# Two mixers paced more slowly, their columns read out by ScalarE, and four products moved ahead of the points where they must end

## The chip, the core and the metric

One Trainium2 chip, one of its cores. The metric is the device time of one execution of the whole program in microseconds (us), median of three runs.

## The reference

Two transformer-like blocks over 256 tokens of width 2048, all in float32. Only the first half of the first block matters here:

```
h = rms_norm(x, mix_norm)
u, q, f, i, og, cx, v, o, ig, fg, gates = split(h @ w_in)
y_a = s5_mixer(u, ...)                 # linear recurrence in 32 groups of 64 complex states, GELU, GLU
y_b = hgrn2_mixer(q, f, i, og, ...)    # gated linear attention, 6 heads of 128
y_c = mlstm_mixer(cx, v, o, ig, fg, ...)
merged = sigmoid(g_a) * (y_a @ wb_a) + sigmoid(g_b) * (y_b @ wb_b) + sigmoid(g_c) * (y_c @ wb_c)
x = x + merged @ w_out                 # then the feed-forward part, and the second block
```

In `hgrn2_mixer`, `q` becomes `silu(q)`, `f` becomes `lb + (1 - lb) * sigmoid(f)`, `k = 1 - f`, and `log f` is summed over time.

## The kernel before

**Products.** Every large product streams its weights from HBM in tiles of 128 x 1024 (two blocks of 128 rows by 512 columns). ScalarE rounds a tile to `hi`, VectorE takes `lo = raw - hi`, and TensorE runs the product in three parts (`mmA` and `mmB`, L362 to L380). One tile is one step of a product. Each of `raw`, `hi` and `lo` has three buffers, and the tile of step s + 2 is split while step s is multiplied. A product accumulates in one of two PSUM buffers called `mm`.

**The order.** Everything is written into the engines' instruction streams in a fixed order; each engine runs its own stream in order. `block1` runs these products: the columns of S5 and the first 512 of HGRN2 together (16 steps, the list `first`), two more products for the HGRN2 columns `q` and `f` (8 steps each), then HGRN2's values and gate (`nat("w_b")`, 24 steps), mLSTM's columns (`w_b` 8 and `w_c` 8 steps), then the merge gates by column block c and branch b (`gates(c)`, three products of 8 steps), `nat("w_d")` (24), and the branch products (`branch(c, b)`, 2 steps for S5's branch, 3 for the others). Numbered from the first, step 32 ends the HGRN2 columns, step 72 ends `w_c`, step 96 ends `gates(0)`, step 144 ends `w_d`. A step of `w_c` has tiles of 584 columns.

**Background.** The three mixers are Python generators. After each step `bg.pump()` lets them write some of their instructions between the products. How much is set by two meters that add up planned costs for VectorE and ScalarE (no measured times), every instruction of the engine counted, those of the products too:

```
RATE, CAP = 2.6, 2
self.V = Meter(nc.vector, 0.066, 1.042e-3, 0.13)   # fixed, per element of a row, extra below 100
self.S = Meter(nc.scalar, 0.2, 0.84e-3)
self.cv = min(self.cv + self.rate - (self.vec.t - self.seen[0]), CAP)   # in pump; ca alike
while self.cv > 0 and self.ca > 0:                 # the first task in the list that is ready
```

A generator's `yield` ends a piece; `yield 1` or `yield 2` gives up that many pumps; `yield self.hold("m2")` waits for a PSUM buffer (`m2` has one, `m1` two). The list of tasks is in the order S5's constants, S5, HGRN2 (short tasks that finish a product go ahead of them), so HGRN2 gets what S5 leaves. `bg.finish(task)` writes all the rest of a task at that point, without regard to the credit: nothing of the next product stands between those instructions.

**S5** (`s5`, from L722): four groups g of two halves. One half is four small products into `s5px` (L742), seven pieces on VectorE (twelve operations on 128 x 512 and four scans on 128 x 256) and products into `s5py` (L775, L776). GpSimd builds the tables of cosines and sines (`s5_table`), of which group g + 1 is asked for when group g begins. At the end come a GELU, the GLU product (`s5g`, L790) with weights loaded by a DMA of GpSimd's queue into two buffers of the pool `a4`, a sigmoid and `ya`. `bg.finish(t_s5)` stands after `gates(0)`, at step 96.

**HGRN2** (`hg`, from L811): the gates' arithmetic; two diagonal products (L849); seven levels for block lengths 1 to 64, each with an Exp on ScalarE, up to four operations on VectorE and two groups of products (L878); then the part across 128 tokens (L900), the output (L914, L915), a norm per head, and transposes (L948) that give `yb`. `bg.finish(t_hg)` stands after `nat("w_d")`, at step 144. mLSTM starts when HGRN2 has ended.

**The first columns.** `first[1]`, in one of the two `mm` buffers, and the next product are multiplied by the tokens' factor `R` (1 / rms) straight out of PSUM on VectorE, after `bg.finish(t_st)`, where the factor is there.

Of the kernel before, what the change touches and what calls it, by code (L numbers as in the profile page):

```python
# [11 lines left out]
AF = mybir.ActivationFunctionType  # L12
OP = mybir.AluOpType
# [5 lines left out]
class Meter:  # L19


    def __init__(self, eng, fixed, per, chain=0.0):
        self.eng, self.fixed, self.per, self.chain, self.t = eng, fixed, per, chain, 0.0

    def __getattr__(self, name):
        f = getattr(self.eng, name)

        def call(*a, **k):
            n = 1
            for x in (*a, *k.values()):  # L30
                if hasattr(x, "shape"):
                    m = 1
                    for d in x.shape[1:]:
                        m *= d
                    n = max(n, m)
            self.t += self.fixed + self.per * n + (self.chain if n < 100 else 0.0)
            return f(*a, **k)  # L37

        return call
# [503 lines left out]
class Mixers(Net):  # L543
# [60 lines left out]
    def s5_consts(self, a4f):  # L604

        V, nc = self.V, self.nc
        s = lambda k, n=16: self.p5.tile([128, n], F32, name=k)
        bc = a4f([128, 1024], F32, "s5bc")
        bt, ct = bc[:, 0:512], bc[:, 512:1024]
        lr, li = self.col("lam_re"), self.col("lam_im")  # L610
        yield 4
        dt = yield from self.exp16(self.col("log_dt"), "dt")
        lrd, th, den, t, ar, ai, cr, ci = (s(k) for k in ("lrd", "th", "den", "t16", "ar", "ai", "cr", "ci"))
        V.tensor_mul(th, li, dt)
        V.tensor_mul(lrd, lr, dt)
        yield
        cs, sn = yield from self.sincos(th, self.p5, [128, 16], "sc")
        mag = self.mag = yield from self.exp16(lrd, "mag")
        yield
        self.nc.sync.dma_start(bt, self.A["s5_b"])  # L620
        self.nc.sync.dma_start(ct, self.A["s5_c"])
        V.tensor_mul(t, lr, lr)
        V.tensor_mul(den, li, li)
        V.tensor_add(den, den, t)
        V.reciprocal(den, den)
        ex = a4f([128, 2, 16, 32], F32, "s5ex")
        cc = self.s5cc = a4f([128, 2, 16, 32], F32, "s5cc")
        self.G.memset(ex, 0.0)
        self.G.memset(cc, 0.0)
        yield 2  # L630
        V.tensor_mul(ar, mag, cs)
        V.tensor_mul(ai, mag, sn)
        V.tensor_scalar(ar, ar, -1.0, None, op0=OP.add)
        V.tensor_mul(cr, ar, lr)
        V.tensor_mul(t, ai, li)
        V.tensor_add(cr, cr, t)
        V.tensor_mul(cr, cr, den)
        V.tensor_mul(ci, ai, lr)
        V.tensor_mul(t, ar, li)
        V.tensor_sub(ci, ci, t)  # L640
        V.tensor_mul(ci, ci, den)
        yield

        self.pw = s("pw", 256).rearrange("p (z k n) -> p z k n", z=2, k=8)
        V.tensor_copy(self.pw[:, 0, 0], cs)
        V.tensor_copy(self.pw[:, 1, 0], sn)
        t2 = s("t162")
        for k in range(7):
            if k % 3 == 0:
                yield  # L650
            c, z = self.pw[:, 0, k], self.pw[:, 1, k]
            V.tensor_mul(t, c, c)
            V.tensor_mul(t2, z, z)
            V.tensor_sub(self.pw[:, 0, k + 1], t, t2)
            V.scalar_tensor_tensor(self.pw[:, 1, k + 1], c, 2.0, z, op0=OP.mult, op1=OP.mult)
        self.s5_base()
        self.s5_t0 = self.s5_table(0)
        yield

        b4 = bt.rearrange("p (z n q) -> p z n q", z=2, n=16)  # L660
        c4 = ct.rearrange("p (z n q) -> p z n q", z=2, n=16)
        t1 = s("s5t", 256).rearrange("p (n q) -> p n q", n=16)
        for g in range(2):
            h = slice(g * 64, g * 64 + 64)
            q = slice(g * 16, g * 16 + 16)
            crb = cr[h, :, None].to_broadcast([64, 16, 16])
            cib = ci[h, :, None].to_broadcast([64, 16, 16])
            V.tensor_mul(ex[h, 0, :, q], b4[h, 0], crb)
            V.tensor_mul(t1[h], b4[h, 1], cib)
            V.tensor_sub(ex[h, 0, :, q], ex[h, 0, :, q], t1[h])  # L670
            yield
            V.tensor_mul(ex[h, 1, :, q], b4[h, 1], crb)
            V.tensor_mul(t1[h], b4[h, 0], cib)
            V.tensor_add(ex[h, 1, :, q], ex[h, 1, :, q], t1[h])
            V.tensor_copy(cc[h, 0, :, q], c4[h, 0])
            V.tensor_scalar(cc[h, 1, :, q], c4[h, 1], -1.0, None, op0=OP.mult)
        bb = self.s5bb = a4f([128, 2, 4, 128], F32, "s5bb")
        for z in range(2):
            yield self.hold("m1")
            ps = self.m1([128, 4, 128])  # L680
            for g in range(4):
                nc.tensor.transpose(ps[:, g], ex[:, z, 4 * g:4 * g + 4].rearrange("p a b -> p (a b)"), self.ident)
            yield 1
            V.tensor_copy(bb[:, z], ps)
            self.drop("m1")
# [36 lines left out]
    def s5(self, u):  # L722

        V, S, nc = self.V, self.S, self.nc
# [5 lines left out]
        for g in range(4):  # L730
            if g < 3:
                tabs[g + 1] = self.s5_table(g + 1)
            C, Sn = tabs.pop(g)
            yield self.hold("m1")
            py = self.m1([128, 256], "s5py")
            for hf in range(2):
# [8 lines left out]
                c, s = C[:, 2 * hf:2 * hf + 2], Sn[:, 2 * hf:2 * hf + 2]  # L745
# [11 lines left out]
                for j in range(2):  # L757
                    p = 4 * g + 2 * hf + j
# [13 lines left out]
                for j in range(2):  # L772
                    q = (2 * hf + j) * 32
                    p = 4 * g + 2 * hf + j
# [33 lines left out]
    def a6(self, shape, dt=F32, name="a6"):  # L808
        return self.a6p.tile(shape, dt, tag="a6", name=name)

    def hg(self, qr, fr):  # L811
        V, S, G, nc = self.V, self.S, self.G, self.nc
        lb, om = self.small([128, 6], "lb"), self.small([128, 6], "om")

        src = self.col("hg_lb")
# [13 lines left out]
        V.memset(kh, 0.0)  # L829
        yield  # L830
        for h in range(6):
            V.tensor_scalar(fr[:, h], fr[:, h], om[:, h:h + 1], lb[:, h:h + 1], op0=OP.mult, op1=OP.add)
        yield
        k = self.a6([128, 6, 256], name="hgk")
        V.tensor_scalar(k, fr, -1.0, 1.0, op0=OP.mult, op1=OP.add)
        yield
        V.tensor_scalar(fr, fr, 1e-19, None, op0=OP.max)
        S.activation(fr, fr, AF.Ln)
        P = fr
# [3 lines left out]
        for t in range(2):  # L843
# [3 lines left out]
            ps = self.m2([128, 6, 128])  # L847
# [6 lines left out]
        for j, b in enumerate((1, 2, 4, 8, 16, 32, 64)):  # L854
# [19 lines left out]
            for t in range(2):  # L874
                yield self.hold("m1")
                ps = self.m1([128, 6, 64])
# [21 lines left out]
        ps = self.m2([128, 6, 128])  # L898
# [9 lines left out]
        for t in range(2):  # L908
            yield self.hold("m2")
            ps = self.m2([128, 6, 128])  # L910
# [183 lines left out]
class Block1(Mixers):  # L1094
# [14 lines left out]
    def order(self):  # L1109

        p = self.plan
# [5 lines left out]
        p("w_c", 0, 8, w=292)  # L1117
        p("w_g", 0, 48)
        p("w_d", 0, 24)
        for c in range(4):  # L1120
            if c > 1:
                p("w_g", 24 * c, 24)
            p("w_br", 5 * c, 5)
        p("w_br", 20, 12)
        pp = self.pair_plan
# [52 lines left out]
    def block1(self):  # L1178
# [9 lines left out]
        X = XT(self)  # L1188
# [73 lines left out]
        def s5():  # L1262
            yield lambda: t_st[3]
            V.tensor_mul(u, first[0], Rb(4))
            self.drop("m2")
            yield from self.s5(u)

        t_s5 = bg.add(s5())
        qr = self.a6([128, 6, 256], name="hgq")
        fr = self.a6([128, 6, 256], name="hgf")  # L1270
        ps = self.prodA("w_a", X, 16)
        bg.finish(t_st)
        r, R = st["r"], st["R"]
        V.tensor_mul(qr[:, 0:4], first[1], Rb(4))
        V.tensor_mul(qr[:, 4:6], ps[:, 0:2], Rb(2))
        V.tensor_mul(fr[:, 0:2], ps[:, 2:4], Rb(2))
        ps = self.prodA("w_a", X, 16)
        V.tensor_mul(fr[:, 2:6], ps, Rb(4))
        self.hg_v = self.hg_gate = self.ml_v = self.ml_gate = None
        t_hg = bg.add(self.hg(qr, fr))  # L1280


        def nat(name, fn, make, row, done):
# [39 lines left out]
        ps = self.prodA("w_b", X, 16)  # L1323
# [14 lines left out]
        for z in range(2):  # L1338
            V.tensor_mul(gt[0:4, z], ps[32 * z:32 * z + 4, 2], R[32 * z:32 * z + 4])

        def gates(c):
            out = []
            for b in range(3):
                ps = self.prodB("w_g", X, 16)
                g = self.a4([128, 2, 512], name="gate")
                for t in range(2):
                    S.activation(g[:, t], ps[:, t], AF.Sigmoid, scale=r[:, t:t + 1])
                out.append(g)
            return out

        def branch(c, b):

            yh, yl = getattr(self, ("ya", "yb", "yc")[b])
            ps = self.prodB("w_br", lambda k: (yh[:, k], yl[:, k]), (4, 6, 6)[b])
            V.tensor_mul(g[c][b], ps, g[c][b])
        g = [gates(0)]
        bg.finish(t_s5)
        s5p.close()
        lp = mixp.enter_context(tc.tile_pool(name="late", bufs=1, reuse_waits="tile"))
        self.late = lambda shape, name: lp.tile(shape, F32, name=name)  # L1360
        t_ml = bg.add(self.ml(cx, gt, lambda: t_hg[3]))
        g.append(gates(1))
        nat("w_d", None, self.late, "ml_norm", ml_done)
        bg.finish(t_hg)
        for c in range(4):
            if c > 1:
                g.append(gates(c))
            for b in range(2):
                branch(c, b)
            G.tensor_add(g[c][0], g[c][0], g[c][1])  # L1370
            g[c][1] = None
        bg.finish(t_ml)
# [808 lines left out]
```

## Time and profile before

| | us |
|---|---|
| median of three runs | 3503.44 (3500.94 to 3505.87) |
| the profiled execution, its own time | 3505.45 |
| its span, first to last instruction | 3503.6 |

The span is what the views below show; the profiled execution's time lies 1.85 us above it. Times in a view are from the span's start. Matmul ends are modelled, so what counts for TensorE is when instructions start and what it waited for. In the names of tiles buffer numbers are left out, and every VectorE and ScalarE instruction has the helper's line L37, so these go by tile: `lo<-raw,hi` is the split of a weight tile, `mm` a product's PSUM tile, `m` a small PSUM tile.

### The profile page before, as it was taken

How to read it: one execution, taken by the hardware profiler on the slowest of the kernel's cores; microseconds unless marked ns; L12 is line 12 of the kernel's file. 1: busy time of each engine (PE TensorE's matmuls, PEld its weight loads, DVE VectorE, ACT ScalarE, POOL GpSimd, SP SyncE). 2: the span in 40 equal slices, each digit the busy share in tenths (PEclk: the TensorE clock that was granted, in tenths of full speed). 3: DMA queues.
4: the chain of work that ended last, by engine and by line, in shares of the span. 5: the costliest groups of instructions: out<-in, count | busy, mean ns of one | idle time of the engine just before them, and what ended most of it. 6: DMA issues, size and time to landing. Idle time of an engine off the chain costs nothing.

```text
span 3503.6 us, 47474 instructions
## 1 busy us (share of the span) xinstructions
PE 3465.1 (99%) x18330; PEld 2976.7 (85%) x18330; DVE 2426.0 (69%) x3216; ACT 1717.5 (49%) x2103; POOL 240.6 (7%) x288
## 2 busy tenths in 40 slices
PE   8999999999999999999999999999999999999999
PEld 8788888888888888888888889988888888888887
DVE  7897575566776577657769998876666666666665
ACT  4435543445554455555554456654444444444454
POOL 5520000000000000003203000000000000000000
PEclk9999999999999999999999999999999999999999
DMA  7444554565566555665555556667666666667765
GB/s 236 149 148 163 176 176 140 194 207 184 188 198 199 186 192 193 192 192 180 159 163 178 183 182 209 214 195 214 202 202 202 203 202 201 202 202 216 217 186 180
DMA packets 236314, 665.85 MB, mean 190 GB/s; under 512 B 77956, under 2 KB 78404, under 8 KB 234168
## 3 DMA queue, kind: packets, MB, share of 16 engines
q1 hardware_dynamic: 230952, 637.49, 57.1%
q10 hardware_dynamic: 2448, 15.22, 1.4%
q0 software_dynamic: 2688, 10.12, 1.0%
q8 instruction: 143, 2.34, 0.3%
q14 instruction: 83, 0.68, 0.1%
HBM read 645.97 MB, written 16.78 MB: 189 GB/s over the span
## 4 chain that ended last, share of the span: by engine, by line
PE 92%; DVE 4%; DMA 1%; issue 1%; ACT 0%; DVEq 0%; ACTq 0%
PE mm L362 33%; PE mm L393 23%; PE mm L366 16%; PE mm L395 12%; PE mm L377 2%; DVE lo L37 2%; PE m L2028 2%; PE mm L380 1%; DMA raw<-in_w_u_dram 1%; PE m L496 1%; PE m L878 0%; DVE s L37 0%; PE m L1038 0%; DVE cand L37 0%; DVE e L37 0%
## 5 line engine op out<-in xcount | busy, mean ns | idle before, releaser
L37 DVE TENSOR_TENSOR lo<-raw,hi 128x1024 fp32r<-128x1024 f32 (+1 forms) x1169 | 1428.5, 1228 | 754.3 <-ACT hi L37 748.2
L37 ACT ACTIVATE hi<-raw 128x1024 fp32r<-128x1024 f32 (+1 forms) x1185 | 1245.3, 1054 | 1290.3 <-PE mm L362 716.9
L393 PE MATMUL mm<-xt,hi 128*128 128x512 f32 x3712 | 898.6, 392 | 0.0
L393 PEld LDWEIGHTS mm<-xt,hi 128*128 128x128 f32 x3712 | 679.5, 188 | 129.0
L395 PEld LDWEIGHTS mm<-xt,lo 128*128 128x128 f32 x3712 | 478.1, 191 | 21.0 <-DVE lo L37 2.9
L395 PE MATMUL mm<-xt,lo 128*128 128x256 f32 x3712 | 491.2, 284 | 2.0 <-DVE lo L37 2.0
L362 PE MATMUL mm<-hi,wl 128*128 128x512 f32 x1024 | 400.0, 391 | 1.9 <-DVE wl L37 1.9
L362 PE MATMUL mm<-hi,wh 128*128 128x512 f32 x928 | 361.6, 390 | 0.0
L362 PE MATMUL mm<-hi,x 128*128 128x512 f32 x1152 | 289.7, 394 | 1.0 <-ACT hi L37 1.0
L362 PEld LDWEIGHTS mm<-hi,x 128*128 128x128 f32 x1152 | 213.5, 188 | 48.8 <-issue 3.9
L366 PE MATMUL mm<-lo,wh 128*128 128x512 f32 x928 | 248.2, 389 | 0.0
L362 PEld LDWEIGHTS mm<-hi,wl 128*128 128x128 f32 x1024 | 193.1, 189 | 42.1 <-DVE wl L37 2.2
L362 PEld LDWEIGHTS mm<-hi,wh 128*128 128x128 f32 x928 | 174.3, 188 | 36.1
L366 PEld LDWEIGHTS mm<-lo,wh 128*128 128x128 f32 x928 | 174.2, 188 | 36.1
L362 PE MATMUL mm<-hi,xt 128*128 128x512 f32 x752 | 186.9, 391 | 0.1
L37 DVE TENSOR_TENSOR resid<-resid,mm 128x1024 f32<-128x1024 f32 x84 | 102.5, 1220 | 99.3 <-PE mm L366 99.3
L362 PEld LDWEIGHTS mm<-hi,xt 128*128 128x128 f32 x752 | 140.4, 188 | 29.2 <-issue 0.5
L366 PE MATMUL mm<-lo,x 128*128 128x512 f32 x576 | 155.1, 391 | 5.5 <-DVE lo L37 5.5
L362 PE MATMUL mm<-hi,acth 128*128 128x512 f32 x352 | 137.3, 390 | 0.0
L362 PE MATMUL mm<-hi,actl 128*128 128x512 f32 x352 | 137.0, 389 | 0.0
L366 PEld LDWEIGHTS mm<-lo,x 128*128 128x128 f32 x576 | 107.6, 188 | 30.7 <-DVE lo L37 8.5
L366 PE MATMUL mm<-lo,xt 128*128 128x512 f32 x376 | 100.6, 389 | 0.0
(566 smaller groups left out, 3530.1 us busy)
## 6 DMA issues: line engine op xcount, KB each, us to landing
raw<-in_w_u_dram SPq DMA_DIRECT2D x256, 512.0 KB, 4.1
raw<-in_w_v_dram SPq DMA_DIRECT2D x256, 512.0 KB, 4.2
raw<-in_w_up_dram SPq DMA_DIRECT2D x176, 512.0 KB, 4.0
raw<-in_w_g_dram SPq DMA_DIRECT2D x96, 512.0 KB, 3.3
raw<-in_w_dn_dram SPq DMA_DIRECT2D x88, 512.0 KB, 3.4
raw<-in_w_o_dram SPq DMA_DIRECT2D x64, 512.0 KB, 3.4
raw<-in_w_b_dram SPq DMA_DIRECT2D x32, 512.0 KB, 3.5
raw<-in_w_br_dram SPq DMA_DIRECT2D x32, 512.0 KB, 3.4
```

The lines of the kernel that those rows point to most:

```text
L37: return f(*a, **k)
L362: nc.tensor.matmul(ps[:, t, :n], x[:, t * 128:t * 128 + 128], hi[:, i, :n], start=first and i == z == 0, stop=False)
L366: nc.tensor.matmul(ps[:, t, :n], X(k0 + i)[0][:, t * 128:t * 128 + 128], lo[:, i, :n], start=False, stop=last and i == kk - 1)
L377: nc.tensor.matmul(ps[:, c, :], hi[:, i, sl[c]], x, start=first and i == z == 0 and c % 2 == 0, stop=False, **kw)
L380: nc.tensor.matmul(ps[:, c, :], lo[:, i, sl[c]], X(k0 + i)[0], start=False, stop=last and i == kk - 1, **kw)
L393: nc.tensor.matmul(ps[:, c], hi[:, i, sl[c]], X.both(k0 + i), start=first and i == 0, stop=last and i == kk - 1, **kw)
L395: nc.tensor.matmul(ps[:, c, 256:], lo[:, i, sl[c]], X(k0 + i)[0], start=False, stop=False, **kw)
L496: self.nc.tensor.transpose(ps[:, c, t * 128:t * 128 + 128], src(t)[:, c * 128:c * 128 + 128], self.ident)
L2028: nc.tensor.matmul(ps[n][:, i], AB[:, 1, i], AB[:, 0, i], start=True, stop=True)
```

## The change

HGRN2's columns leave PSUM by ScalarE copies without the factor; `hg` multiplies them by `R` in SBUF as its first two pieces. The affine of `f` (six operations) and `k = 1 - f` go from VectorE to ScalarE. The meter of VectorE counts every cost 1.3 times from the end of the powers in `s5_consts` until S5's group 3 begins. Two products of `gates(1)` (16 steps) move ahead of `bg.finish(t_s5)`, and `branch(0, 0)` and `branch(1, 0)` (2 steps each) ahead of `bg.finish(t_hg)`; the weights' stream in `order` follows.

```diff
--- before.py
+++ after.py
@@ -21,6 +21,7 @@
 
     def __init__(self, eng, fixed, per, chain=0.0):
         self.eng, self.fixed, self.per, self.chain, self.t = eng, fixed, per, chain, 0.0
+        self.k = 1.0
 
     def __getattr__(self, name):
         f = getattr(self.eng, name)
@@ -33,7 +34,7 @@
                     for d in x.shape[1:]:
                         m *= d
                     n = max(n, m)
-            self.t += self.fixed + self.per * n + (self.chain if n < 100 else 0.0)
+            self.t += self.k * (self.fixed + self.per * n + (self.chain if n < 100 else 0.0))
             return f(*a, **k)
 
         return call
@@ -653,6 +654,7 @@
             V.tensor_mul(t2, z, z)
             V.tensor_sub(self.pw[:, 0, k + 1], t, t2)
             V.scalar_tensor_tensor(self.pw[:, 1, k + 1], c, 2.0, z, op0=OP.mult, op1=OP.mult)
+        V.k = 1.3
         self.s5_base()
         self.s5_t0 = self.s5_table(0)
         yield
@@ -730,6 +732,8 @@
         for g in range(4):
             if g < 3:
                 tabs[g + 1] = self.s5_table(g + 1)
+            else:
+                V.k = 1.0
             C, Sn = tabs.pop(g)
             yield self.hold("m1")
             py = self.m1([128, 256], "s5py")
@@ -808,8 +812,12 @@
     def a6(self, shape, dt=F32, name="a6"):
         return self.a6p.tile(shape, dt, tag="a6", name=name)
 
-    def hg(self, qr, fr):
+    def hg(self, qr, fr, Rb):
         V, S, G, nc = self.V, self.S, self.G, self.nc
+        V.tensor_mul(fr, fr, Rb(6))
+        yield
+        V.tensor_mul(qr, qr, Rb(6))
+        yield
         lb, om = self.small([128, 6], "lb"), self.small([128, 6], "om")
 
         src = self.col("hg_lb")
@@ -829,11 +837,11 @@
         V.memset(kh, 0.0)
         yield
         for h in range(6):
-            V.tensor_scalar(fr[:, h], fr[:, h], om[:, h:h + 1], lb[:, h:h + 1], op0=OP.mult, op1=OP.add)
+            S.activation(fr[:, h], fr[:, h], AF.Identity, scale=om[:, h:h + 1], bias=lb[:, h:h + 1])
         yield
         k = self.a6([128, 6, 256], name="hgk")
-        V.tensor_scalar(k, fr, -1.0, 1.0, op0=OP.mult, op1=OP.add)
-        yield
+        S.activation(k, fr, AF.Identity, scale=-1.0, bias=1.0)
+        yield 1
         V.tensor_scalar(fr, fr, 1e-19, None, op0=OP.max)
         S.activation(fr, fr, AF.Ln)
         P = fr
@@ -1117,9 +1125,12 @@
         p("w_c", 0, 8, w=292)
         p("w_g", 0, 48)
         p("w_d", 0, 24)
-        for c in range(4):
-            if c > 1:
-                p("w_g", 24 * c, 24)
+        p("w_br", 0, 2)
+        p("w_br", 5, 2)
+        p("w_br", 2, 3)
+        p("w_br", 7, 3)
+        for c in (2, 3):
+            p("w_g", 24 * c, 24)
             p("w_br", 5 * c, 5)
         p("w_br", 20, 12)
         pp = self.pair_plan
@@ -1266,18 +1277,19 @@
             yield from self.s5(u)
 
         t_s5 = bg.add(s5())
+
         qr = self.a6([128, 6, 256], name="hgq")
         fr = self.a6([128, 6, 256], name="hgf")
+        S.activation(qr[:, 0:4], first[1], AF.Copy)
         ps = self.prodA("w_a", X, 16)
+        S.activation(qr[:, 4:6], ps[:, 0:2], AF.Copy)
+        S.activation(fr[:, 0:2], ps[:, 2:4], AF.Copy)
+        ps = self.prodA("w_a", X, 16)
+        S.activation(fr[:, 2:6], ps, AF.Copy)
         bg.finish(t_st)
         r, R = st["r"], st["R"]
-        V.tensor_mul(qr[:, 0:4], first[1], Rb(4))
-        V.tensor_mul(qr[:, 4:6], ps[:, 0:2], Rb(2))
-        V.tensor_mul(fr[:, 0:2], ps[:, 2:4], Rb(2))
-        ps = self.prodA("w_a", X, 16)
-        V.tensor_mul(fr[:, 2:6], ps, Rb(4))
         self.hg_v = self.hg_gate = self.ml_v = self.ml_gate = None
-        t_hg = bg.add(self.hg(qr, fr))
+        t_hg = bg.add(self.hg(qr, fr, Rb))
 
 
         def nat(name, fn, make, row, done):
@@ -1338,9 +1350,9 @@
         for z in range(2):
             V.tensor_mul(gt[0:4, z], ps[32 * z:32 * z + 4, 2], R[32 * z:32 * z + 4])
 
-        def gates(c):
+        def gates(c, bs=range(3)):
             out = []
-            for b in range(3):
+            for b in bs:
                 ps = self.prodB("w_g", X, 16)
                 g = self.a4([128, 2, 512], name="gate")
                 for t in range(2):
@@ -1353,20 +1365,22 @@
             yh, yl = getattr(self, ("ya", "yb", "yc")[b])
             ps = self.prodB("w_br", lambda k: (yh[:, k], yl[:, k]), (4, 6, 6)[b])
             V.tensor_mul(g[c][b], ps, g[c][b])
-        g = [gates(0)]
+        g = [gates(0), gates(1, range(2))]
         bg.finish(t_s5)
         s5p.close()
         lp = mixp.enter_context(tc.tile_pool(name="late", bufs=1, reuse_waits="tile"))
         self.late = lambda shape, name: lp.tile(shape, F32, name=name)
         t_ml = bg.add(self.ml(cx, gt, lambda: t_hg[3]))
-        g.append(gates(1))
+        g[1] += gates(1, range(2, 3))
         nat("w_d", None, self.late, "ml_norm", ml_done)
+        branch(0, 0)
+        branch(1, 0)
         bg.finish(t_hg)
         for c in range(4):
             if c > 1:
                 g.append(gates(c))
-            for b in range(2):
-                branch(c, b)
+                branch(c, 0)
+            branch(c, 1)
             G.tensor_add(g[c][0], g[c][0], g[c][1])
             g[c][1] = None
         bg.finish(t_ml)
```

## Rows read from the trace of the kernel before

**Rows 1.** The page's part 1: engine, busy us, share of the span, instructions.

```profile
PE 3465.1 (99%) x18330; PEld 2976.7 (85%) x18330; DVE 2426.0 (69%) x3216; ACT 1717.5 (49%) x2103; POOL 240.6 (7%) x288
```

**Rows 2.** Windows, all engines: length, busy of each, then PEclk, DMA share, GB/s.

```profile
82.15:85.19 3.04, 0.00 (x1) 0.03 (x1) 3.04 (x4) 0.00 (x0) 2.96 (x4) 0.88 0.26 94
85.19:93.69 8.50, 8.50 (x49) 8.50 (x49) 4.34 (x5) 1.82 (x2) 8.34 (x9) 0.64 0.38 103
112.65:158.40 45.75, 39.17 (x171) 28.92 (x169) 41.35 (x46) 17.90 (x19) 27.76 (x29) 1.00 0.42 136
158.40:195.93 37.53, 37.01 (x180) 28.77 (x180) 32.92 (x45) 19.57 (x22) 0.00 (x0) 1.00 0.57 184
195.93:247.90 51.97, 49.17 (x407) 46.12 (x405) 48.98 (x61) 17.68 (x20) 22.48 (x26) 1.00 0.43 128
```

**Rows 3.** Timeline of TensorE, 85 to 139 us: start, length, group, idle before it.

```profile
85.19 3.76 PE L377 MATMUL mm<-x,hi 128*128 128x256 f32 x16 [3.04 <-DVE hgq L37]
...
104.01 2.08 PE L377 MATMUL mm<-x,hi 128*128 128x256 f32 x16
...
106.89 2.08 PE L377 MATMUL mm<-x,hi 128*128 128x256 f32 x16
...
138.90 1.19 PE L366 MATMUL mm<-lo,x 128*128 128x512 f32 x4 [1.69 <-DVE lo L37]
```

**Rows 4.** Timeline of TensorE: S5's first half, its last group and its end.

```profile
99.97 1.14 PE L742 MATMUL s5px<-u,s5bb 32*128 32x256 f32 x8
...
273.90 1.14 PE L742 MATMUL s5px<-u,s5bb 32*128 32x256 f32 x8
...
318.29 0.63 PE L775 MATMUL s5py<-s5sr,s5cc 128*32 128x256 f32 x4
...
323.04 7.17 PE L790 MATMUL s5g<-s5y,glu 128*128 128x256 f32 x32 [0.71 <-ACT s5y L37]
```

**Rows 5.** Timeline of TensorE: HGRN2's levels 4 and 64, its last transposes.

```profile
335.52 1.45 PE L878 MATMUL m<-hgqh,hgkh 128*128 128x64 f32 x12
...
400.91 1.45 PE L878 MATMUL m<-hgqh,hgkh 128*128 128x64 f32 x12
...
453.65 0.60 PE L948 MATMUL m<-cols,hgo 128*128 128x128 f32 x4
```

**Rows 6.** One S5 half on VectorE: all instructions of the window, then `lo` alone.

```profile
250.21:266.05 15.84, 15.67 (x21) 1.00 0.54 170
...
250.21:266.05 15.84, 6.07 (x5) 1.00 0.54 170
```

**Rows 7.** Groups by form on VectorE, 401 to 456 us: count, busy, mean ns.

```profile
L37 DVE TENSOR_TENSOR hgnq<-hgo 128x1536 f32<-128x1536 f32 x1 | 1.8, 1751 | 0.0
...
L37 DVE TENSOR_TENSOR hgqh<-hgqh,hgq 128x768 f32<-128x768 f32 x1 | 0.9, 950 | 0.0
...
L37 DVE SCALAR_TENSOR_TENSOR hgny<-hgnt,hgny 128x12 f32<-128x12 f32 x3 | 0.5, 171 | 0.1
```

**Rows 8.** Groups by form on ScalarE, 401 to 456 us.

```profile
L37 ACT ACTIVATE hgo<-m 128x768 f32<-128x768 f32 x2 | 1.6, 812 | 3.7 <-PE m L915 3.7
```

**Rows 9.** Timeline of VectorE, 119 to 160 us.

```profile
119.60 1.22 DVE L37 TENSOR_TENSOR hgf<-mm,R 128x1024 f32<-128x1024 f32 x1
...
134.03 2.83 DVE L37 TENSOR_TENSOR hgq<-hgq,hgkh 128x1536 f32<-128x1536 f32 x1
...
158.19 2.02 DVE L37 TENSOR_SCALAR hgf<-hgf,om,lb 128x256 f32<-128x256 f32 x6
```

**Rows 10.** Timeline of ScalarE, S5's GELU and its sigmoid.

```profile
321.93 1.06 ACT L37 ACTIVATE s5y<-s5y 128x1024 f32<-128x1024 f32 x1 [2.08 <-DVE s5y L37]
...
330.25 1.56 ACT L37 ACTIVATE s5z<-s5g,cols 128x256 f32<-128x256 f32 x4 [4.69 <-PE s5g L790]
```

**Rows 11.** DMA issues, 280 to 330 us: count, KB, median us to landing.

```profile
glu<-in_w_glu_dram POOLq DMA_DIRECT2D x2, 512.0 KB, 5.3
```

## The prediction, made before the change was run

> **What bounds the kernel now.** I read the page's part 1 first: TensorE is busy 99% of the span [rows 1], so a change around the mixers moves the time only where TensorE waits for them. The windows of the first 480 us then show where that is. TensorE is idle 3.04 us at 82.15, runs the next 8.50 us at a mean clock of 0.64, and is idle 6.58, 0.52 and 2.80 us in the three windows from 112.65 to 247.90 (length less busy) [rows 2]. The timeline says for what: at 85.19 the fourth product waited for `hgq`, VectorE's multiplication that empties the PSUM buffer; at 138.90 it waited for `lo`, the split that VectorE delivers late [rows 3]. After that it waits 0.71 us for the GELU at S5's end [rows 4], and from there to the feed-forward part it is dense. VectorE is the second limit up to 247.90: 41.35 of 45.75 us and 48.98 of 51.97 us are busy, while ScalarE has more than half of its time free [rows 2].
>
> The clock's price comes from the same rows. A step of this kind takes 2.88 us (104.01 to 106.89) [rows 3]; the two steps from 85.19 took 8.50 us in place of 5.76, so the half-clock stretch behind a 3.04 us idle cost 2.74 us [rows 2].
>
> What the change can win is thus 3.04 + 2.74 = 5.8 us at the first columns, and at most 6.58 + 0.52 + 2.80 + 0.71 = 10.6 us of waits after them: 16.4 us in all.
>
> **The first columns.** ScalarE's copies need no `R`, so the buffer is free some 25 us before the fourth product wants it. The 3.04 us wait goes and the clock stays up: 5.8 us, the surest term. Four copies (two of 1024, two of 512 columns, together about 3.4 us as an estimate from the 0.81 us for 768 columns [rows 8]) lie on an engine with room. VectorE loses its four multiplications out of PSUM (1.22 us for 1024 columns [rows 9]; two of 1024 and two of 512 make about 3.7), the six affine operations (2.02 us) and `k`, and gains two multiplications of 128x1536 in SBUF, 1.75 us each at the price of `hgnq` [rows 7]. Such an operation took 2.83 us at 134.03 [rows 9], where GpSimd was busy 27.76 of 45.75 us [rows 2], so the two cost 3.5 to 5.7 us. None of this changes the sum: VectorE is a little lighter either way. The Trainium skill's GPSIMD Engine Reference (Specifications) says that VectorE shares its SBUF interfaces with GpSimd, with contention for instructions that have two SBUF inputs; that speaks against this part, since the new multiplications have two and the old ones had one, and the 2.83 us agrees. By it these would cost 5.7 us. The skill's ScalarE: Activation LUTs (Rules for kernel authors) would keep multiplications and additions on VectorE; per operation of 256 columns, ScalarE took 1.56 / 4 = 0.39 us [rows 10] against VectorE's 2.02 / 6 = 0.34 [rows 9], so the rule holds by a hair, and what counts here is which engine is late.
>
> **The pacing.** The meter's costs say only which instruction is written behind which step; I use them for the order, and rows for every duration. One split of 1024 columns counts 0.066 + 1.042e-3 x 1024 = 1.133, so of 2.6 per step 1.467 is left for background. One S5 half is twelve operations of 512 (0.600 each) and four scans of 256 (0.333): 8.53, that is 5.8 steps, and its yields give up three more: 8.8 steps. The trace agrees: the first half's products stand behind step 28 (99.97), those of group 3 behind step 81 (273.90) [rows 4], 53 steps for six halves. With the factor 1.3 the split counts 1.473, leaving 1.127, and a half counts 11.09: 9.8 + 3 = 12.8 steps. The first half still starts near step 29 (the constants are two steps slower; the three multiplications written at step 24 are gone). Six halves later it is step 29 + 77 = 106. From there the factor is 1.0, and the last group's halves take 8.8 steps each: they end at steps 115 and 124. `finish(t_s5)` now stands at 96 + 16 = 112. Working the credit forward step by step, debts and HGRN2's pieces included, gives the same: the last group begins at step 107, its first half's last piece is written in step 112, and the whole second half is written by `finish`.
>
> HGRN2 gets what S5 leaves, which is little until then: by the same working it stands between its two diagonal products at step 112, while before it was already at level 4 behind step 98 (335.52) [rows 5]. A level takes five steps because of its yields: 335.52 to 400.91 is four levels, 16.35 us each [rows 5]. Seven levels from step 115 on last until 150; `finish(t_hg)` comes at 112 + 8 + 24 + 4 = 148. All that follows the last level, which before was spread from 400.91 to 453.65 [rows 5], is written at once.
>
> **What the two ends cost.** TensorE runs its stream in order, so the next product waits behind the mixer's own small products. VectorE then has no splits to do between.
> S5: one half took 15.84 us, of which splits 6.07 [rows 6], so 9.8 us of its own; then the skip term (0.4, an estimate from the 0.34 above), the GELU 1.06 [rows 10] and four handovers (1.0 with the start, which no row prices): 12.3 us idle. The following sigmoid lies under `s5g` (7.17 us) as before.
> HGRN2: two 128x768 operations (1.9), four of 128x1536 (7.0), twelve of 128x12 (2.1) [rows 7], three ScalarE copies (2.4) [rows 8], the first split of `yb` (1.2, estimated from these rows), handovers 1.5 (not priced either): 16.1 us.
> Each idle is longer than the 3.04 us that was followed by the half clock; I take 2.74 us for each: 5.5.
> Loss: 12.3 + 16.1 + 5.5 = 33.9. Gain: 5.8 + 10.6 less 1.2 for ScalarE's block of two sigmoids, which stays: 15.2. Sum +18.7 us: 3522 on the median; on the profiled execution (3505.45, span 3503.6, 2 us above the median) 3524.
>
> Bounds: the loss is at least VectorE's work on the two chains, 9.8 + 11.0, without clock or handovers: 20.8, and the gain at most 16.4: +4.4. The gain is at least 5.8. The loss is at most 44.7: the GLU weights late by their whole 5.3 us landing [rows 11], because all `a4` buffers are held until S5's last half frees some, and the clock's price twice as high (11). That gives +38.9.
>
> mLSTM starts thirteen steps later; it has 64 steps left to its `finish`, and its output ends well inside the branch products before, so I cost that at nothing. If that cover were gone, a third stall like HGRN2's would follow.
>
> **Rivals.**
> (1) *Both mixers still end before their `finish`* (the moved products cover the slower pace). Then only the gain is left: 3503.4 - 15.2 = 3488. For it: the products moved ahead are 16 and 4 steps of cover. Against it: 12.8 steps per half. It decides if S5's last group starts by step 95, twelve earlier than I work out.
> (2) *One end is covered, the other not*, or the chains overlap with work I count as serial: one loss of about 17 against 15: 3505, no change.
> (3) *The ends are dearer*: GLU weights late, a longer half-clock stretch: +30 and more, 3533 to 3542.
> (4) *The pace relieves nothing*: the `lo` waits stay, because GpSimd stretches VectorE's operations and not the amount of background. Then the gain is 5.8, and the sum +28: 3531. Against it: per step VectorE is asked for 2.0 in place of 2.6 planned us.
>
> **How the numbers follow.** Forecast (slower by 10 to 28 us) 0.62; (3) and (4) together 0.17; (2) 0.10; (1) 0.11. 0.2% is 7 us, about what a measurement of this kernel can tell from no change. Slower 0.79, same 0.10, faster 0.11. The range leaves out (1) and the far end of (3): 3507 (the lower bound) to 3537.
>
> **What would show it.** No TensorE idle and clock 1.0 between the third and fourth product; fewer `lo` waits from 110 to 250 us. Behind the fifth gate product: `s5px` (L742), a gap near 10 us, `s5py`, a gap near 2, `s5g`. Behind the second branch product: L878, L900, L914 and L915 with gaps, a gap near 11 us, L948. The clock at half behind both. If S5's last L742 group has product steps behind it before `s5g`, my count of steps is wrong, and with it the sign.

## The result, and the profile after

The changed kernel took 3527.39 us (median of six, 3525.39 to 3535.17), the kernel before 3504.18 in the same comparison: ratio 1.0071, 95% interval 1.0061 to 1.0081. It is slower by some 23 us; 18.7 were forecast. The profiled execution was the longest of the six: 3535.17 us, span 3533.4, mean granted clock 0.990, where the other five show 0.993 and 3525.4 to 3528.6. What follows accounts for the profiled one.

TensorE's timeline of the changed kernel where the fourth product begins (start, length, then line and operation):

```profile
79.28 1.12 PE L381 MATMUL mm<-x,lo 128*128 128x256 f32 x8
80.24 2.08 PE L378 MATMUL mm<-x,hi 128*128 128x256 f32 x16
82.16 1.12 PE L381 MATMUL mm<-x,lo 128*128 128x256 f32 x8
```

The wait for `hgq` [rows 3] and the half clock behind it are gone: the product step that stood at 112.65 us [rows 2] stands at 105.40. From there to 341 us only one wait for `lo` is left, where three windows and the GELU wait of the kernel before made 10.6 us [rows 2, 4]:

```profile
117.47 1.97 PE L367 MATMUL mm<-lo,x 128*128 128x512 f32 x4 [1.91 <-DVE lo L38]
```

Then come the two ends. First S5's, behind the fifth gate product:

```profile
341.28 0.40 PE L780 MATMUL s5py<-s5si,s5cc 128*32 128x256 f32 x1 [1.25 <-DVE s5si L38]
...
342.27 1.14 PE L746 MATMUL s5px<-u,s5bb 32*128 32x256 f32 x8
351.84 1.06 PE L779 MATMUL s5py<-s5sr,s5cc 128*32 128x256 f32 x2 [8.44 <-DVE s5sr L38]
353.89 0.64 PE L780 MATMUL s5py<-s5si,s5cc 128*32 128x256 f32 x1 [0.99 <-DVE s5si L38]
...
357.48 10.07 PE L794 MATMUL s5g<-s5y,glu 128*128 128x256 f32 x32 [1.66 <-ACT s5y L38]
367.19 2.20 PE L363 MATMUL mm<-hi,x 128*128 128x512 f32 x8
...
373.84 2.11 PE L363 MATMUL mm<-hi,x 128*128 128x512 f32 x8 [0.81 <-ACT hi L38]
```

No product step stands between the last half's `s5px` and `s5g`. Then HGRN2's, behind the second branch product:

```profile
484.92 2.86 PE L886 MATMUL m<-hgqh,hgkh 128*128 128x64 f32 x24 [0.45 <-DVE hgkh L38]
491.63 2.93 PE L908 MATMUL m<-hgqh,hgkh 128*128 128x128 f32 x12 [3.84 <-DVE hgkh L38]
495.46 2.93 PE L923 MATMUL m<-natv,hgA 128*128 128x128 f32 x12 [0.90 <-ACT hgX L38]
499.34 0.79 PE L922 MATMUL m<-natv,hgX 128*128 128x128 f32 x2 [0.96 <-ACT hgo L38]
...
514.70 1.97 PE L956 MATMUL m<-cols,hgo 128*128 128x128 f32 x8 [10.53 <-DVE hgo L38]
517.23 1.11 PE L956 MATMUL m<-cols,hgo 128*128 128x128 f32 x4 [0.56 <-DVE ybl L38]
517.99 0.77 PE L363 MATMUL mm<-hi,ybh 128*128 128x512 f32 x1
```

The bracketed waits sum to 13.15 and 17.24 us. The windows of the changed kernel show the clock there (busy us of TensorE, its weight loads, VectorE, ScalarE, GpSimd, then the mean granted clock, the DMA share and GB/s):

```profile
105.40:200.00 94.60, 92.69 (x494) 77.71 (x493) 81.45 (x83) 44.27 (x47) 64.78 (x62) 0.98 0.55 169
200.00:341.00 141.00, 140.02 (x724) 114.56 (x722) 108.69 (x132) 62.46 (x69) 0.00 (x0) 1.00 0.55 176
341.00:367.20 26.20, 14.83 (x55) 9.83 (x55) 10.88 (x18) 2.19 (x2) 1.12 (x2) 0.67 0.17 59
484.00:520.60 36.60, 19.36 (x94) 17.12 (x93) 19.35 (x29) 6.75 (x9) 1.62 (x3) 0.63 0.19 61
```

The granted clock has two levels, full and half, so a mean of 0.67 over 26.2 us is 17 us at the lower level (26.2 x 0.33 x 2), and 0.63 over 36.6 us is 27 us.

### The profile page after: what moved, and what is told of

It is laid out like the page before. It is cut to its first block, busy times and chain, and to the rows that moved or that the text cites. A ratio compares the mean times of both kernels' runs of the same rounds, so it can differ in the third digit from the quotient of the medians.

```text
span 3533.4 us, 47485 instructions
## 1 busy us (share of the span) xinstructions
PE 3476.8 (98%) x18330; PEld 2984.7 (84%) x18330; DVE 2428.5 (69%) x3207; ACT 1727.2 (49%) x2116; POOL 249.6 (7%) x288
## 4 chain that ended last, share of the span: by engine, by line
PE 95%; DVE 3%; DMA 1%; ACT 0%; issue 0%; SPq 0%; DVEq 0%; ACTq 0%
PE mm L363 33%; PE mm L394 23%; PE mm L367 16%; PE mm L396 12%; PE mm L378 3%; PE m L2042 2%; PE mm L381 1%; DVE lo L38 1%; PE m L497 1%; PE m L886 0%; PE m L1046 0%; DMA raw<-in_w_a_dram 0%; PE s5g L794 0%; PE m L378 0%; PE s5px L746 0%
## 5 line engine op out<-in xcount | busy, mean ns | idle before, releaser
L367 PE MATMUL mm<-lo,wh 128*128 128x512 f32 x928 | 248.0, 389 | 0.0
L367 PEld LDWEIGHTS mm<-lo,wh 128*128 128x128 f32 x928 | 174.2, 188 | 36.1
L367 PE MATMUL mm<-lo,x 128*128 128x512 f32 x576 | 156.2, 393 | 2.3 <-DVE lo L38 2.2
L367 PEld LDWEIGHTS mm<-lo,x 128*128 128x128 f32 x576 | 108.7, 189 | 26.8 <-DVE lo L38 4.1
L367 PE MATMUL mm<-lo,xt 128*128 128x512 f32 x376 | 100.5, 389 | 0.0
```

The costliest lines, as they stand in the source:

```text
L367: nc.tensor.matmul(ps[:, t, :n], X(k0 + i)[0][:, t * 128:t * 128 + 128], lo[:, i, :n], start=False, stop=last and i == kk - 1)
```

## The experiments

Each run is given with its median and its ratio to the kernel before (95% interval).

**The parts by themselves.** Run pace_off, the changed kernel with `V.k = 1.0` in place of 1.3:

> The changed kernel with the factor 1.0 in place of 1.3; copies through ScalarE and moved products stay. My theory (the loss is what the slower pace leaves for the two ends): by the kernel's own meter S5 is wholly written at step 98 of 112 and HGRN2 at 136 of 148, so nothing is written at once at either end, both idle stretches (13 and 17 us) and the half clock behind them go, and the first columns' gain of about 7 us stays, with some lo waits back: about 3496 us, 3490 to 3500. Rival A (the copies or the moved products cost something themselves, through held buffers or late GLU weights): the time stays above 3510 with the ends covered. Rival B (the pace is what pays for the gain ahead of S5): 3504, as before.

3503.63 us, 1.0002 (0.9993 to 1.0011). The loss is gone, so it hangs on the factor. But the gain is gone as well: rival B. Its TensorE waits as in the next run, up to 4.40 us ahead of L367 at 148.51.

Run evac_only, the copies and HGRN2's ScalarE operations alone:

```
+        V.tensor_mul(fr, fr, Rb(6))
...
-            V.tensor_scalar(fr[:, h], fr[:, h], om[:, h:h + 1], lb[:, h:h + 1], op0=OP.mult, op1=OP.add)
+            S.activation(fr[:, h], fr[:, h], AF.Identity, scale=om[:, h:h + 1], bias=lb[:, h:h + 1])
...
+        S.activation(qr[:, 0:4], first[1], AF.Copy)
...
-        V.tensor_mul(qr[:, 0:4], first[1], Rb(4))
```

> The kernel before with one part alone: HGRN2's columns leave PSUM through ScalarE, with the affine operations and k on ScalarE; no pacing factor, no moved products. My theory: the wait ahead of the fourth product and its half clock go, all else as before: 3504 less 6 to 8, about 3497. Rival A (two multiplications with two SBUF inputs beside GpSimd, and six more operations on ScalarE, slow what follows): 3503 or more, with longer lo waits from 110 to 250 us.

3504.03 us, 1.0000 (0.9991 to 1.0009): the copies by themselves win nothing. TensorE is 7.2 us ahead at the step that stood at 106.89 [rows 3], and behind again at 165. Its timeline in between:

```profile
136.71 1.75 PE L366 MATMUL mm<-lo,x 128*128 128x512 f32 x4 [2.29 <-DVE lo L37]
...
148.71 2.08 PE L366 MATMUL mm<-lo,x 128*128 128x512 f32 x4 [4.40 <-DVE lo L37]
...
155.33 3.78 PE L362 MATMUL mm<-hi,x 128*128 128x512 f32 x8 [2.68 <-ACT hi L37]
```

Why VectorE is late with the two `lo` is in its own timeline:

```profile
137.72 1.52 DVE L37 TENSOR_TENSOR s<-s5i,s5S 128x512 f32<-128x512 f32 x1
139.16 2.06 DVE L37 TENSOR_TENSOR lo<-raw,hi 128x1024 fp32r<-128x1024 f32 x1
141.15 1.77 DVE L37 TENSOR_TENSOR s5sr<-s,s 128x512 f32<-128x512 f32 x1
```

The same operations take 0.68, 1.22 and 0.68 us where GpSimd rests (run notab_evac, below):

```profile
126.44 0.68 DVE L37 TENSOR_TENSOR s<-s5i,s5S 128x512 f32<-128x512 f32 x1
127.05 1.22 DVE L37 TENSOR_TENSOR lo<-raw,hi 128x1024 fp32r<-128x1024 f32 x1
128.18 0.68 DVE L37 TENSOR_TENSOR s5sr<-s,s 128x512 f32<-128x512 f32 x1
```

The third wait, for `hi`, comes from VectorE too: ScalarE stands idle for 13.00 us until VectorE's `lb` is there, and has 5.4 us of other work ahead of the next `hi` (148.80 to 154.22). The six affine operations that the change gave to ScalarE begin at 161.24, behind that wait, and are not its cause.

```profile
148.80 0.21 ACT L37 ACTIVATE lb<-lb 128x6 f32<-128x6 f32 x1 [13.00 <-DVE lb L37]
```

The window from 140 to 170 us, first of the kernel before, then of evac_only:

```profile
140.00:170.00 30.00, 27.78 (x125) 20.91 (x124) 28.39 (x37) 13.36 (x13) 1.12 (x1) 1.00 0.54 174
```

```profile
140.00:170.00 30.00, 22.92 (x84) 16.10 (x83) 23.64 (x23) 14.36 (x18) 29.22 (x31) 0.76 0.37 114
```

GpSimd is busy 29.22 of 30 us in place of 1.12. In the kernel before, GpSimd's timeline shows it idle for 62.36 us ahead of the table of group 3 (released by VectorE's `natg`), which begins at 203.48; with the copies it follows the table of group 2 at once, from 146.88. First the kernel before, then evac_only:

```profile
203.48 1.17 POOL L717 COPY s5C<-s5Cb 128x64 f32<-128x64 f32 x1 [62.36 <-DVE natg L37]
```

```profile
146.88 0.69 POOL L717 COPY s5C<-s5Cb 128x64 f32<-128x64 f32 x1
```

Run moves_only, the two gate and two branch products moved, nothing else:

```
-        g = [gates(0)]
+        g = [gates(0), gates(1, range(2))]
         bg.finish(t_s5)
...
+        branch(0, 0)
+        branch(1, 0)
         bg.finish(t_hg)
```

> The kernel before with one part alone: two gate products ahead of S5's end and two branch products ahead of HGRN2's, with their weights' order. My theory: both mixers already end in time, so only the 0.71 us wait at S5's GELU can go: 3502 to 3505, no change. Rival A (the moved products cost, through buffers held longer or GLU weights that land late): 3508 or more, with a wait ahead of s5g.

3501.85 us, 0.9995 (0.9986 to 1.0004): no change, as expected.

Run pace_evac, the changed kernel without its moved products:

> The changed kernel without its moved products: factor 1.3 and the copies stay. By the meter, 31.2 planned us of VectorE work are then written at once at S5's end in place of 11.1, and at HGRN2's end 2 to 4 in place of 13.6. My theory (the loss follows what is written at once): S5's end idle 13 + 20 x 1.1 = about 35 us with more small products at half clock, HGRN2's end almost closed: about 3534, 3522 to 3545, with several groups L746, gap, L779 and gap behind the third gate product. Rival (the moved products themselves make the loss): back to about 3500.

3537.09 us, 1.0097 (1.0081 to 1.0112). As expected: three halves are written at once at S5's end, with the same gap each time.

```profile
299.55 1.06 PE L779 MATMUL s5py<-s5sr,s5cc 128*32 128x256 f32 x2 [8.44 <-DVE s5sr L38]
...
314.03 1.06 PE L779 MATMUL s5py<-s5sr,s5cc 128*32 128x256 f32 x2 [8.49 <-DVE s5sr L38]
...
328.45 1.06 PE L779 MATMUL s5py<-s5sr,s5cc 128*32 128x256 f32 x2 [8.43 <-DVE s5sr L38]
```

A half written at once takes 14.4 us from one to the next. HGRN2's end shrinks to a wait of 3.22 us ahead of L956.

**How slow a pace, and for how long.** Runs pace_1_1 and pace_1_2 change the factor; pace_g1 ends it two groups earlier:

```
-            else:
+            if g == 1:
                 V.k = 1.0
```

> The changed kernel with the factor 1.1. By the meter S5 is done at step 106 of 112 and HGRN2 just at 148, nothing written at once. My theory: part of the lo waits goes, no stall at the ends: 3496 us, 3490 to 3501. Rival (a factor this small leaves VectorE as late as with 1.0): 3503.

> The changed kernel with the factor 1.2. By the meter 2.3 planned us are written at once at S5's end (as in the kernel before) in place of 11.1, and 7.6 at HGRN2's in place of 13.6. My theory (the loss follows what is written at once): S5's 13 us idle and its half clock, about 4.5, go, HGRN2's 17 us become about 10: 3527 less 13, 4.5 and 7, about 3502; 3497 to 3508. Rival (the loss belongs to the moved products or the buffers, and not to the count of steps): above 3515.

> The changed kernel, with the factor 1.3 set back to 1.0 at the start of S5's second group in place of its last. By the meter nothing is then written at once at S5's end (S5 is done at step 107 of 112) and 0.6 planned us at HGRN2's. My theory (the factor wins by thinning VectorE's list while GpSimd builds S5's tables, and loses only by what it leaves for the ends): the lead of some 16 us that the changed kernel had at step 57 is kept but for a few later waits: 3491 us, 3486 to 3498, faster than both kernels. Rival (work put off only waits later: what the pace wins is given back as lo waits behind the reset): about 3503.

- pace_1_1: 3499.24 us, 0.9990 (0.9981 to 0.9999). Inside the range of my theory, 3 us above its centre; no stall at the ends, but eight waits from 110 to 190 us, 9.4 us in all.
- pace_1_2: 3514.28 us, 1.0034 (1.0022 to 1.0047). Neither: my 3502 was wrong. HGRN2's end idles 8.9 us, near the 10 expected, but I had carried over the gain of the factor 1.3 (a wait of 3.58 us ahead of L367 at 149.71 is back, with the half clock), and the stretch ahead of S5's end was not free: a first-level product of HGRN2, L886, held TensorE 3.29 us at 342.17, and the clock fell behind it (0.66 over the next 9.8 us).
- pace_g1: 3495.74 us, 0.9978 (0.9969 to 0.9987), the lowest median of the kernels here that leave no work out (that of no_copies_1_1, below, lies inside its interval). It keeps some 7 us of the 12 expected. Its profiled execution was its longest, 3502.02 us. Nothing stalls at S5's end, TensorE's timeline shows `s5g` ahead of time:

```profile
328.40 0.63 PE L779 MATMUL s5py<-s5sr,s5cc 128*32 128x256 f32 x4
...
339.10 7.07 PE L794 MATMUL s5g<-s5y,glu 128*128 128x256 f32 x32
```

Part of the rival holds, though: behind the reset waits are back, the longest 2.76 us ahead of L746 at 231.15, with half clock after it.

**Whether GpSimd is the reason.** Runs notab_before and notab_evac fill S5's tables of groups 1 to 3 with a constant, in the kernel before and in evac_only:

```
+        if g:
+            self.G.memset(C, 0.5)
+            self.G.memset(S, 0.5)
+            return C, S
```

> The kernel before, with S5's tables of groups 1 to 3 filled with a constant (two GpSimd operations each) in place of GpSimd's 26 operations each; S5's values are thus not the reference's, VectorE's and TensorE's work is unchanged. My theory (the lo waits from 110 to 160 us come from GpSimd's table, during which VectorE's two-input operations take up to twice as long): most of the 6.6 us of waits goes: 3504 less 5 to 7, about 3498. Rival (VectorE is late by the amount of its work, whoever runs beside it): 3502 or more.

> As the run above, with the copies through ScalarE and HGRN2's affine operations there. My theory: without GpSimd beside VectorE the 7 us of the first columns are no longer given back between 100 and 170 us: 3491, 3487 to 3495, some 7 below the run above. Rival (VectorE is saturated by its own work): the same time as the run above.

3492.17 us, 0.9965 (0.9953 to 0.9978), and 3486.03 us, 0.9952 (0.9938 to 0.9965). Leaving out the three tables is worth 11 us in the kernel before, more than the 5 to 7 that I expected. With GpSimd at rest the copies are worth 6.1 us by the medians, near the 5.8 of the prediction: the fastest execution of notab_before (3489.28) is slower than the slowest of notab_evac (3488.53). Beside GpSimd's tables they are worth nothing. The windows from 105 to 200 us, of evac_only, then of notab_evac:

```profile
105.00:200.00 95.00, 81.79 (x347) 61.80 (x347) 88.20 (x90) 37.24 (x43) 64.53 (x62) 0.91 0.45 143
```

```profile
105.00:200.00 95.00, 93.66 (x514) 77.55 (x513) 84.08 (x106) 48.42 (x54) 0.95 (x1) 1.00 0.54 174
```

VectorE does 106 operations in less time than 90 took. Run no_copies_1_1 is pace_1_1 without the copies:

> The factor 1.1 and the moved products, without the copies through ScalarE. By the meter nothing is written at once at S5's end and 0.6 planned us at HGRN2's. Its pair with the copies took 3499. My theory (beside a thinner VectorE list the copies win what they should): the wait ahead of the fourth product is back with its half clock: 3504, 3501 to 3507. Rival (the copies win nothing here either): 3499.

3497.79 us, 0.9983 (0.9974 to 0.9992). My expectation was wrong; at the factor 1.1 the copies still win nothing. The wait for `hgq` is back, but from 85 to 190 us this kernel waits 8.5 us in all, where pace_1_1 waits 9.4. And the half clock behind that wait, which I had counted in, is not there:

```profile
85.23 2.14 PE L378 MATMUL mm<-x,hi 128*128 128x256 f32 x16 [3.42 <-DVE hgq L38]
```

```profile
85.23:93.70 8.47, 8.46 (x71) 8.47 (x72) 6.20 (x6) 2.65 (x3) 8.31 (x6) 1.00 0.50 148
```

The granted clock is 1.00 behind 3.42 us of idle, where the kernel before had 0.64 behind 3.04 us [rows 2]. The factor 1.3 without the copies was not tried.

**The clock at the ends.** Run fill puts products of no use into the idle stretches, fill_half half as many:

```
+                if g == 3 and hf == 1:
+                    for _ in range(34):
+                        nc.tensor.matmul(py[64:128], C[:, 1, 0:64], C[:, 0], start=True, stop=True, skip_group_check=True)
...
```

> The changed kernel with products whose results are not used put into the two idle stretches: 34 of 64x256 columns ahead of S5's last four, 14 of 128x256 ahead of HGRN2's half product and 42 of 128x256 ahead of its first transposes, each written into the PSUM buffer that the next real product then overwrites. The waits stay; TensorE is busy in them. My theory (the half clock follows TensorE's idleness and is paid on the products behind it): granted clock 1.0 through both ends, s5g back from 10.07 to about 7.2 us, 8 to 11 us gained: about 3518, 3514 to 3521. Rival (those products at half clock lay inside the waits for VectorE anyway, so the clock costs nothing): 3527.

> As the run fill, with half as many products, since each was two passes there and they overran the waits: 18, 8 and 23, by the trace of that run 7.9, 3.6 and 10.0 us for idle stretches of 8.4, 3.8 and 10.5. My theory (the half clock follows TensorE's idleness and is paid on the products behind it, about 4.5 us at S5's end and 6 to 7 at HGRN2's): 3516, 3513 to 3520, clock 1.0 through both ends. Rival (the products at half clock cost nothing because they lie inside waits for VectorE): 3527.

fill took 3535.44 us, 1.0091 (1.0076 to 1.0106), because the products overran the waits; it shows the clock all the same. TensorE's timeline of fill:

```profile
342.08 14.89 PE L778 MATMUL s5py<-s5C 128*64 128x256 f32 x68
...
359.65 7.17 PE L797 MATMUL s5g<-s5y,glu 128*128 128x256 f32 x32 [1.68 <-ACT s5y L38]
```

`s5g` is back from 10.07 to 7.17 us. fill_half took 3523.90 us, 1.0060 (1.0046 to 1.0074). Its windows:

```profile
341.00:367.20 26.20, 22.58 (x97) 16.18 (x96) 11.72 (x18) 3.91 (x6) 1.12 (x2) 0.93 0.12 40
480.00:510.00 30.00, 25.77 (x155) 22.50 (x155) 18.22 (x28) 6.54 (x9) 1.61 (x3) 1.00 0.23 75
```

At HGRN2's end the clock stays up. From L886 to the first product of `ybh` it is 27.74 us (480.53 to 508.27) against 33.07 in the changed kernel, and the eight products of one step behind take 1.93 against 3.04: 6.4 us. At S5's end the gaps that were left still brought some 3.7 us of half clock (26.2 x 0.07 x 2), and `s5g` took 8.86. By the medians fill_half wins only 3.5 us, where I expected 11, and its interval overlaps that of the changed kernel. The profiled execution of the changed kernel had more half clock than its other five (0.990 against 0.993), so its price of the clock is not that of the median, which no trace shows.

## Why the prediction came out as it did

**The sign and the place** were right, step for step: two ends not covered, the waits at the named lines, half clock behind both, the last half of S5 written at once. pace_off shows that the factor causes it, pace_evac that the loss follows what is left to write; rivals (1) and (2) are out, and rival (3)'s late weights too, since `s5g` waited for `s5y`; its longer half-clock stretch is what the trace shows. Rival (4) is refuted for the changed kernel: with the factor only one `lo` wait is left.

**The loss** was sized too small for the profiled execution. Idle: 13.15 and 17.24 us for 12.3 and 16.1 forecast. The clock was the mis-sized term. I took 2.74 us for each end, the price of a 3.04 us idle [rows 2]. That one row is no constant: behind the same wait for `hgq`, no_copies_1_1 kept the full clock. The idle stretches here are several waits in a row with small products between, and the clock stayed down for 17 and 27 us. At S5's end that is 2.90 on `s5g` and 1.3 on the products of `s5py` behind the gap (1.06 and 1.93 us against 0.62 and 1.05 in fill_half), 4.2; at HGRN2's 6.4. Together the two ends cost some 13.15 + 4.2 + 17.24 + 6.4 = 41.0 us in the profiled execution, for 33.9.

**The gain** follows: the product matmul that stood at 664.9 us stands at 692.8, so as a remainder it was 41.0 - 27.9 = 13.1 us, for 15.2 forecast. Of the 10.6 us of waits in the kernel before, 2.3 were for `hgA` and 1.0 for ScalarE's `hi`, and not for `lo`; they went with the rest. What remains to the span's 29.8 are 1.9 us in the second block, with its own half-clock stretches. In the other executions of the changed kernel some 8 us less are lost; where, no trace shows. If all of it were the clock at the two ends, they would have paid some 3 us for it (4.2 + 6.4 less 7.8), under the 5.5 of the forecast; so the clock is shown to be mis-sized for the profiled execution alone. The median lies 4.5 us above the forecast.

**The step that failed** is the account of where the gain comes from, though its sum came near: "5.8 us, the surest term" for the copies, and "None of this changes the sum" for the two-input multiplications and GpSimd. The terms do not add up. (ScalarE's price was low too: its six affine operations took 3.05 us at 241.09 of the changed kernel, 0.51 each, where the sigmoid's row had given 0.39.) While GpSimd builds tables VectorE sets the pace of the product steps, so a TensorE that comes 7 us earlier only waits longer for `lo`. evac_only shows it (0), notab_before against notab_evac shows the reason (6.1 without the tables). The copies also let the table of group 3 start 56.6 us earlier, beside VectorE's list; the trace shows that, no run took it apart. The gain of the changed kernel needs the pace: pace_off has the copies without it and wins nothing. Whether it needs the copies is not shown: at the factor 1.1 the pace wins as much without them.

The Trainium skill's GPSIMD Engine Reference (Specifications) says that GpSimd shares its SBUF interfaces with VectorE, with contention for VectorE instructions that have two SBUF inputs. The trace of evac_only agrees: 0.68 us became 1.52 and 1.77, 1.22 became 2.06. I had read the rule as a price on two multiplications. VectorE's multiplications of `s5px`, which read one input from PSUM, kept their 0.68 us beside a busy GpSimd, and the addition of two SBUF tiles next to them did not:

```profile
167.94 0.68 DVE L37 TENSOR_TENSOR s<-s5px,s5S 128x512 f32<-128x512 f32 x1
168.66 1.21 DVE L37 TENSOR_TENSOR s5r<-s,s 128x512 f32<-128x512 f32 x1
```

Not every operation of the kind was stretched: a split at 126.95 took its 1.22 us while GpSimd worked on tiles of 128x128.

## What to carry to other kernels

A wait removed ahead of a stretch that another engine limits is not won; look first which engine sets the pace of the next stretch, and whose work stretches its operations there. Background work that is thinned has to be counted to the point where it must be done: a factor of 1.3 over one group was worth 7 us (pace_g1), over the first three it cost 23. And a stretch of several waits can cost more clock than one short wait, since the small products between them run at the lower level too: 4.2 and 6.4 us at the two ends of the profiled execution, against 2.74 us or nothing behind the wait for `hgq`.

## What the runs showed of the hardware that I had not expected

- VectorE's operations with two SBUF inputs took as much as 2.6 times as long while GpSimd worked (1.77 against 0.68 us for 128x512, evac_only against notab_evac), those with one input in PSUM the same 0.68 us; in 95 us it did 90 operations in 88.2 us of busy time beside GpSimd and 106 in 84.1 without.
- Products of operands in plain f32 stand twice in the trace: 34 written, 68 rows of 0.22 us. S5's own small products show the same (two written at L779, x4 in the trace), which I could have read before.
- TensorE's clock stayed at 1.0 through a stretch that useless products filled up to waits of 0.34 to 0.97 us (fill_half at HGRN2's end), and fell for some 3.7 us where 0.52, 1.44 and 1.66 us stayed open between short products (at S5's). Behind the wait for `hgq` it fell after 3.04 us in the kernel before and stayed at 1.00 after 3.42 us in no_copies_1_1, so the length of one wait did not settle it.
